# A two-layer encoder trunk with eight experts: passes of 1024 inner features in place of 512, 4096 B rows of gate and up, and banks of sums handed out by count

## The chip, the cores and the metric

The program runs on one core of one Trainium2 chip. The metric is the device time of one execution in microseconds (us), the median over runs; lower is better. A profiled execution gives the trace, from which all rows below are taken.

## The reference

256 tokens of 1024 features pass through two layers in float32. The even layer is a convolution and pooling mixer, then a dense SwiGLU; the odd layer a gated convolution and a spatial gating unit, then eight experts, of which each token takes its best two. All that the change touches lies in the experts:

```python
def swiglu(x, w_gate, w_up, w_down):
    return (jax.nn.silu(x @ w_gate) * (x @ w_up)) @ w_down

def moe_swiglu(x, router, w_gate, w_up, w_down):
    t = x.reshape(-1, d)                                   # 256 x 1024
    top_logits, top_idx = lax.top_k((t @ router).astype(jnp.float32), TOP_K)
    top_w = jax.nn.softmax(top_logits, axis=-1)
    gates = jnp.sum(jax.nn.one_hot(top_idx, N_EXPERTS) * top_w[..., None], axis=1)
    for e in range(N_EXPERTS):                             # w_gate[e], w_up[e]: 1024 x 3584, w_down[e]: 3584 x 1024
        out = out + gates[:, e:e + 1] * swiglu(t, w_gate[e], w_up[e], w_down[e])
```

Behind each sub-layer stand a scaled residual and a layer norm.

## The kernel before

The weights of the experts are 352 MB, read once. They come in chunks of 1 MiB, in the order of a list `plan`, one transfer each on SP's queue (line 133), into a ring of eight buffers named `raw`; the first twenty or so find room in other tiles too and are loaded while the odd layer still computes. A chunk is used in two halves, and its buffer comes free when its last reader is done.

Experts are taken by rank of their token count, with room for `CAPS` = 64, 160, 128, 128, 64, 64, 64, 64 tokens at ranks 0 to 7. The tokens of one are gathered by matmuls with a selection matrix (`gather`, tiles `S`, `tok`) in blocks of 128 (wide), 64 (narrow) or 32 (slim); rank 1 has a wide and a slim block. Wide blocks work in pairs of reduced-precision numbers: ACT rounds a half chunk (`whi`, line 151), DVE takes the rest (`wlo`, line 158), and three matmuls of 512 columns (`wm`) replace one. Narrow and slim blocks use the raw float32 weights; two narrow matmuls fill the array's columns side by side, or four slim ones. A float32 matmul shows as two records in the trace.

`plan` is a list of items ("g", "u" or "d", rank, f), for gate, up and down of the f-th of seven passes of 512 inner features; an item is two chunks. `STARTS` says in which round each rank begins, so that two or three experts are under way at a time: a round takes the gates of its experts, the downs of the round before and the ups.

`project` multiplies the gathered tokens with gate or up into one bank of sums (PSUM, tag "mm", four banks) per block. Then `shaped` (ACT's Silu at line 1298, DVE's product at 1301) empties the bank, `turned` transposes the product on PE (line 1308, tiles `ident`, `fdk` or `sgate`) and `parted` or `copied` (line 1320) brings it back. These follow-ups are no loop of their own: `later(d, ...)` puts them d ticks on, and every half chunk is one tick (`step`), so that they stand between the matmuls of the next items. `down` multiplies with the down rows into four more banks (tag "acc"), over all passes of a rank; `finish` adds the result to the tokens by matmuls (`scatter`, tiles `fak`, `fcs`) and DVE (line 1431). Slim blocks add two quarters of a bank first (`fek`, lines 1284 and 1285).

Ten items before the end (`IF_AT`) all engines come to a branch (line 1463), taken only if some expert has more tokens than room, which these inputs don't have. Before it all that fits into the ring has been issued. The last rank, 7, is alone at the end; its items there are g, u of f = 4, 5 and 6 and the downs, among them rank 3's last.

Of the kernel before, what the change touches and what calls it, by code (L numbers as in the profile page):

```python
# [35 lines left out]
IF_AT = 10  # L36
CARRY_AT = 1
LAST_CUT = 2
AHEAD = {"ft": (0, 50), "fd": (20, 24), "fa": (2, 18), "fc": (3, 48), "fe": (7, 50), "fb": (8, 56), "f0": (9, 18), "f1": (10, 60)}
# [3 lines left out]
RANK_AT = 3  # L43
# [14 lines left out]
STARTS = ((0, 0), (2, 4), (6, 7), (1, 11), (4, 11), (5, 14), (3, 18), (7, 21))  # L58
# [17 lines left out]
def tile_trunk(ctx: ExitStack, tc: tile.TileContext, a: dict, out: bass.AP, caps=CAPS, starts=STARTS,  # L76
# [149 lines left out]
    NFB = FE // 512  # L226
# [47 lines left out]
    for what, p, f in plan:  # L274
        for h in range(2):
            if not any(n == P for _, n in _blocks(caps[p])):
                plain.update((2 * len(chunks), 2 * len(chunks) + 1))
            if what == "d":
                expert(p, md, f * 512 + h * 256, 256, 0, D)
            else:  # L280
                expert(p, mg if what == "g" else mu, h * 512, 512, f * 512, 512)
# [188 lines left out]
    def aggregate(st):  # L470
        mv = small.tile([P, 2], F32, name="ln_mv")
        ve.bn_aggr(mv, st)
        return mv
# [18 lines left out]
    def unit(t, st, fast):  # L492
# [4 lines left out]
        off = small.tile([P, 1], F32, name="ln_off")  # L497
# [577 lines left out]
    clock = {"n": 0, "free": 0}  # L1075

    def later(d, f, *args):
        events.setdefault(clock["n"] + d, []).append((f, args))

    def tick():  # L1080
        clock["n"] += 1
        for f, args in events.pop(clock["n"], ()):
            f(*args)

    def drain():
        while events:
            tick()

    def step():

        tick()
        n = state["use"]
        return use(), raw_half(n)
# [87 lines left out]
    def gather(p, bi):  # L1181
# [14 lines left out]
        def pick(q):  # L1196
            b = bank()
            for k in range(4):
# [5 lines left out]
            if wide:  # L1204
                later(1, split, xg[:, ks, 0:n], xg[:, ks, n:2 * n], b)
            else:
                later(1, first_picked if (p, bi) == (0, 0) else plain_picked, xg, q, b)

        def flip():
            b = bank()  # L1210
            for t in range(2):
                te.transpose(b[:, t * P:(t + 1) * P], G[:, t, :], ident)
            o = Sg[p, bi] = taker(p, wide)
            later(1, se.activation, o.bitcast(F32) if p == last else o, b[:, :T], AF.Copy)

        later(1, pick, 0)
        later(2, pick, 1)
        if (p, bi) != (0, 0):
            later(4, flip)
# [10 lines left out]
    def row0():  # L1230
        i = nth("row0") % 2
        return late()[:, 512 * i:512 * (i + 1)]

    def over_halves(p, mms):
# [3 lines left out]
        for pair in range(2):  # L1238
            got = [(h,) + step() for h in (2 * pair, 2 * pair + 1)] if len(kinds) > 1 else None
            if got is None:  # L1240
                for h in (2 * pair, 2 * pair + 1):
                    mms[kinds[0]](h, 0, *step())
                continue
            for bi in (1, 0) if pair == 0 else (0, 1):
# [3 lines left out]
    def project(what, p, f):  # L1248
        bs = [bank() for _ in blocks[p]]

        def wide_mm(h, bi, w, raw):
            for j in range(2):
                k = 2 * h + j
                l = Xg[p, bi][:, k, :]
                wm(bs[bi], l[:, 0:P], l[:, P:2 * P], w[0][:, j, :], w[1][:, j, :], k == 0, k == DB - 1)

        def narrow_mm(h, bi, w, raw):

            for j in range(2):
                k = 2 * h + j  # L1260
                for c in range(2):
                    mm(bs[bi][64 * c:64 * c + 64, 0:256], Xg[p, bi][:, k, :], raw[:, j, 256 * c:256 * c + 256],
                       k == 0, k == DB - 1)

        def slim_mm(h, bi, w, raw):


            for j in range(2):
                for c in range(2):
                    at = 64 * j + 32 * c  # L1270
                    mm(bs[bi][at:at + 32, 0:256], Xg[p, bi][:, 2 * h + j, 0:32], raw[:, j, 256 * c:256 * c + 256],
                       h == 0, h == 3)

        over_halves(p, {P: wide_mm, 64: narrow_mm, 32: slim_mm})
        for bi, (base, n) in enumerate(blocks[p]):
            later(1, shaped, p, f, what, bi, bs[bi] if n == P else bs[bi][:, 0:256])

    def shaped(p, f, what, bi, v):
        n = v.shape[1]
        slim = blocks[p][bi][1] == 32  # L1280
        if slim:
            i = 512 + 5 * T * (nth("sums32") % 2)
            t = own()[0:64, i:i + T]
            se.activation(t, v[64:P], AF.Copy)
            ve.tensor_tensor(t, v[0:64], t, op=OP.add)
            v = t
        if what == "g":
            if p == 0:
                s = mop.tile([P, n], F32, name="sgate", bufs=1)
            elif n == 512:  # L1290
                s = row0()
            else:
                i = 4 + nth("sgate") % 4
                s = late()[:, n * i:n * (i + 1)]
            if slim:
                s = s[0:64]
            sgate[p, f, bi] = s
            se.activation(s, v, AF.Silu)  # L1298
            return
        s = sgate.pop((p, f, bi))  # L1300
        ve.tensor_tensor(s, v, s, op=OP.mult)  # L1301
        later(1, turned, p, f, bi, s)

    def turned(p, f, bi, s):
        b = bank()
        m, n = s.shape
        for k in range(n // P):
            te.transpose(b[:, k * m:(k + 1) * m], s[:, k * P:(k + 1) * P], ident[:m, :m])  # L1308
        later(1, parted if n == 512 else copied, p, f, bi, b[:, 0:n // P * m])

    def parted(p, f, bi, v):
        y = mop.tile([P, 4, 2 * P], F32R, name="mh", bufs=2)
        split(y[:, :, 0:P], y[:, :, P:2 * P], v.rearrange("p (k s) -> p k s", k=4))
        mh.setdefault((p, f), {})[bi] = y

    def copied(p, f, bi, v):

        y = part_of(fy, "fb", 8, [256], F32) if p else mop.tile([P, 256], F32, name="mh0", tag="mh", bufs=2)
        y = y[:, 0:v.shape[1]]
        ve.tensor_copy(y, v)  # L1320
        mh.setdefault((p, f), {})[bi] = y
# [3 lines left out]
    def down(p, f):  # L1325
        rows = mh.pop((p, f))
        spill = spills[p]
        for bi, (_, n) in enumerate(blocks[p]):
            if f == 0 or spill[bi]:
                macc[p, bi] = [bank("mm" if spill[bi] else "acc")[:, 0:256 if n == 32 else 512]  # L1330
                               for _ in range(2 if n == P else 1)]

        def ends_of(bi, j):
            return (f == 0 or spill[bi]) and j == 0, (f == NFB - 1 or spill[bi]) and j == 3

        def wide_mm(j, bi, w, raw):
            l = rows[bi][:, j, :]
            for h in range(2):
                s = slice(h * 512, (h + 1) * 512)
                wm(macc[p, bi][h], l[:, 0:P], l[:, P:2 * P], w[0][:, 0, s], w[1][:, 0, s], *ends_of(bi, j))  # L1340

        def narrow_mm(j, bi, w, raw):

            n = blocks[p][bi][1]
            at = (j % 2 * 2 + j // 2) * n
            for c in range(P // n):
                mm(macc[p, bi][0][n * c:n * c + n, :], rows[bi][:, at:at + n], raw[:, 0, 8 * n * c:8 * n * (c + 1)],
                   *ends_of(bi, j))

        over_halves(p, {P: wide_mm, 64: narrow_mm, 32: narrow_mm})  # L1350
        if f == NFB - 1 and p == last:
            return
        for bi in range(len(blocks[p])):
            if spill[bi]:
                later(1, spilled, p, f, bi, macc[p, bi])
# [12 lines left out]
    def finish(p, bi):  # L1368
# [4 lines left out]
        if blocks[p][bi][1] < P:  # L1373
            later(d, settled, p, bi)
            k = 64 // blocks[p][bi][1]
            for i in range(2 * k):
                later(d + 3 + (3 - k) * i, scatter_few, p, bi, i // k, i % k)
            return
        for h in range(2):
            later(d + 4 * h, settle, p, bi, h)  # L1380
            for t in range(2):
                later(d + 4 * h + 3 + t, scatter, p, bi, t, h)
# [31 lines left out]
    def scatter(p, bi, t, h):  # L1414
        b = bank()
        for i, y in enumerate(parts[p, bi, h]):
            mm(b, Sg[p, bi][:, t * P:(t + 1) * P], y, i == 0, i == 1)
        later(1, taken, p, t, half(h), b)

    def scatter_few(p, bi, t, i):  # L1420

        n = blocks[p][bi][1]
        for h in range(2):
            b, c = bank(), 64 // n * h + i
            r, b = slice(n * c, n * c + n), b[:, 0:8 * n]
            mm(b, Sg[p, bi][r, t * P:(t + 1) * P], parts[p, bi][r, :], True, True)
            later(1, taken, p, t, slice(8 * n * c, 8 * n * c + 8 * n), b)
# [6 lines left out]
    at = len(passes)  # L1434
    for n, g in reversed(list(enumerate(passes))):
        for p in [p for p, f in reversed(g) if n and f == 0]:
            at = min(at, n)
            for bi in reversed(range(len(blocks[p]))):
# [176 lines left out]
```

## Time and profile before

| | |
|---|---|
| median of 3 runs (lowest, highest) | 1310.31 us (1309.09, 1310.47) |
| profiled execution: its own time | 1309.43 us |
| its span, first to last instruction | 1307.7 us, mean granted clock 0.986 |
| instructions | 19372 |
| busy share of the span: PE, PEld, DVE, ACT, POOL | 96%, 67%, 55%, 39%, 2% |
| DMA | 421.17 MB, mean 322 GB/s |

PE is TensorE's matmuls, PEld its loads of weights, DVE VectorE, ACT ScalarE, POOL GpSimd, SP the engine that issues the transfers. Busy is time with an instruction at work; the ends of matmuls are modelled, so start-to-start distances say more than durations. PEclk is the granted clock of TensorE, 1.00 for 2.4 GHz and 0.50 for 1.2. The span is 1.7 us shorter than the execution's time, which holds the launch too.

### The profile page before, as it was taken

How to read it: one execution, taken by the hardware profiler on the slowest of the kernel's cores; microseconds unless marked ns; L12 is line 12 of the kernel's file. 1: busy time of each engine (PE TensorE's matmuls, PEld its weight loads, DVE VectorE, ACT ScalarE, POOL GpSimd, SP SyncE). 2: the span in 40 equal slices, each digit the busy share in tenths (PEclk: the TensorE clock that was granted, in tenths of full speed). 3: DMA queues.
4: the chain of work that ended last, by engine and by line, in shares of the span. 5: the costliest groups of instructions: out<-in, count | busy, mean ns of one | idle time of the engine just before them, and what ended most of it. 6: DMA issues, size and time to landing. Idle time of an engine off the chain costs nothing. (4 is left out here: it accounts for less than half of the span.)

```text
span 1307.7 us, 19372 instructions
## 1 busy us (share of the span) xinstructions
PE 1255.8 (96%) x7585; PEld 870.8 (67%) x7585; DVE 712.9 (55%) x1105; ACT 511.9 (39%) x726; POOL 31.8 (2%) x69
## 2 busy tenths in 40 slices
PE   7989999999999999999999999999999999999795
PEld 6848888888777666767765566565556567666451
DVE  4997666667984255555534334434335566544333
ACT  4246555546442144434342233333334244443210
POOL 4000000001000001000000000000000000000000
PEclk8999999999999999999999999999999999999898
DMA  8425755276879999899999999999999999999994
GB/s 294 168 80 177 254 182 178 66 254 194 325 269 345 376 393 394 316 387 393 390 374 345 386 397 378 353 378 390 394 397 394 394 393 394 393 394 394 390 336 174
DMA packets 195803, 421.17 MB, mean 322 GB/s; under 512 B 6816, under 2 KB 43368, under 8 KB 195704
## 3 DMA queue, kind: packets, MB, share of 16 engines
q1 hardware_dynamic: 194200, 414.58, 85.8%
q0 software_dynamic: 1504, 5.28, 1.2%
q8 instruction: 61, 1.00, 0.3%
q14 instruction: 38, 0.31, 0.1%
HBM read 418.78 MB, written 1.05 MB: 321 GB/s over the span
## 5 line engine op out<-in xcount | busy, mean ns | idle before, releaser
L158 DVE TENSOR_TENSOR wlo<-raw,whi 128x1024 fp32r<-128x1024 f32 x354 | 417.4, 1221 | 167.2 <-ACT whi L151 150.2
L151 ACT ACTIVATE whi<-raw 128x1024 fp32r<-128x1024 f32 x354 | 353.1, 1049 | 169.6 <-DMA raw<-in_odd_moe_w_up 72.4
L98 PE MATMUL mm<-whi,xgw 128*128 128x512 f32 x672 | 216.8, 404 | 0.0
L98 PEld LDWEIGHTS mm<-whi,xgw 128*128 128x128 f32 x672 | 122.5, 190 | 44.9 <-issue 15.7
L98 PE MATMUL mm<-raw,f1k 128*64 128x256 f32 (+1 forms) x1344 | 134.4, 386 | 0.0
L98 PE MATMUL mm<-wlo,xgw 128*128 128x512 f32 x336 | 132.2, 393 | 0.3 <-DVE wlo L158 0.3
L98 PE MATMUL mm<-big,whi 128*128 128x512 f32 (+1 forms) x448 | 129.3, 368 | 1.8 <-ACT whi L151 1.8
L98 PE MATMUL mm<-raw,fek 128*64 128x256 f32 x896 | 108.5, 390 | 6.8 <-PEq L1463 6.8
L98 PE MATMUL acc<-whi,mh 128*128 128x512 f32 (+1 forms) x344 | 108.2, 402 | 0.0
L98 PEld LDWEIGHTS mm<-raw,f1k 128*64 128x64 f32 (+1 forms) x1344 | 72.8, 128 | 52.3 <-issue 17.4
L1298 ACT ACTIVATE fdk<-mm 128x256 f32<-128x256 f32 (+1 forms) x49 | 23.2, 473 | 183.1 <-PE mm L98 183.1
L98 PEld LDWEIGHTS mm<-raw,fek 128*64 128x64 f32 x896 | 62.6, 139 | 45.4 <-issue 19.6
L98 PE MATMUL mm<-big,wlo 128*128 128x256 f32 x384 | 92.5, 282 | 0.0
L98 PE MATMUL acc<-raw,fbs 128*64 128x512 f32 (+1 forms) x560 | 91.8, 512 | 0.0
L1301 DVE TENSOR_TENSOR fdk<-mm,fdk 128x256 f32<-128x256 f32 (+1 forms) x49 | 26.4, 538 | 117.9 <-PE mm L98 117.9
L98 PEld LDWEIGHTS mm<-big,whi 128*128 128x128 f32 x448 | 75.1, 193 | 13.3 <-ACT whi L151 2.0
L98 PEld LDWEIGHTS acc<-whi,mh 128*128 128x128 f32 (+1 forms) x344 | 61.9, 187 | 23.8 <-ACT whi L151 10.0
L98 PEld LDWEIGHTS mm<-wlo,xgw 128*128 128x128 f32 x336 | 63.8, 190 | 14.9 <-DVE wlo L158 0.7
L98 PEld LDWEIGHTS mm<-big,wlo 128*128 128x128 f32 x384 | 69.0, 191 | 3.7
L98 PE MATMUL acc<-wlo,mh 128*128 128x512 f32 x168 | 65.5, 390 | 0.0
L98 PEld LDWEIGHTS acc<-raw,fbs 128*64 128x64 f32 (+1 forms) x560 | 28.5, 125 | 52.2 <-issue 48.0
L98 PE MATMUL acc<-whi,ffh 128*128 128x512 f32 x176 | 55.6, 396 | 0.0
(286 smaller groups left out, 1299.6 us busy)
## 6 DMA issues: line engine op xcount, KB each, us to landing
raw<-in_odd_moe_w_gate SPq DMA_DIRECT2D x110, 1024.0 KB, 11.7
raw<-in_odd_moe_w_up SPq DMA_DIRECT2D x110, 1024.0 KB, 11.4
raw<-in_odd_moe_w_down SPq DMA_DIRECT2D x109, 1024.0 KB, 11.5
raw<-in_even_ffn_w_gate SPq DMA_DIRECT2D x11, 1024.0 KB, 5.5
raw<-in_even_ffn_w_up SPq DMA_DIRECT2D x11, 1024.0 KB, 8.2
raw<-in_even_ffn_w_down SPq DMA_DIRECT2D x11, 1024.0 KB, 6.9
raw<-in_odd_w_in SPq DMA_DIRECT2D x10, 1024.0 KB, 14.6
raw<-in_even_w_in SPq DMA_DIRECT2D x5, 1024.0 KB, 9.2
```

The costliest lines, as they stand in the source:

```text
L98: te.matmul(o, lhsT, rhs, start=start, stop=stop)
L151: se.activation(his[n], r, AF.Copy)
L158: ve.tensor_tensor(los[n], r, his[n].bitcast(F32), op=OP.subtract)
L1298: se.activation(s, v, AF.Silu)
L1301: ve.tensor_tensor(s, v, s, op=OP.mult)
```

## The change

Passes take 1024 inner features (`FBLOCKS`: three of 1024 and one of 512), so a rank has four passes instead of seven, and `STARTS` is rewritten in rounds of that length. A chunk of gate or up is 256 rows of 4096 B instead of 512 rows of 2048 B, but in the last pass; chunks stay 1 MiB, and their number and sum stay. An item is four chunks (two in the last pass). A wide block takes two banks in `project`, a narrow one matmuls of 512 columns instead of 256, a slim one too. `later` names the banks that a follow-up will need; it waits in `due` while more than four would be out. The branch stands seven items before the end.

```diff
-IF_AT = 10
+IF_AT = 7
-RANK_AT = 3
+RANK_AT = 1
-STARTS = ((0, 0), (2, 4), (6, 7), (1, 11), (4, 11), (5, 14), (3, 18), (7, 21))
+STARTS = ((0, 0), (2, 2), (6, 4), (1, 6), (4, 6), (5, 8), (3, 10), (7, 12))
+FBLOCKS = ((0, 1024), (1024, 1024), (2048, 1024), (3072, 512))
...
-        for h in range(2):
+        f0, nf = FBLOCKS[f]
+        for h in range(nf // 256):
...
             else:
-                expert(p, mg if what == "g" else mu, h * 512, 512, f * 512, 512)
+                rows = D * 256 // nf
+                expert(p, mg if what == "g" else mu, h * rows, rows, f0, nf)
...
-    def later(d, f, *args):
-        events.setdefault(clock["n"] + d, []).append((f, args))
-
-    def tick():
+    due = deque()
+    def later(d, f, *args, banks=0):
+        events.setdefault(clock["n"] + d, []).append((f, args, banks))
+    def take(n=1):
+        clock["banks"] += n
+        assert clock["banks"] <= 4
+    def frees(f, *args, n=1):
+        def done():
+            f(*args)
+            take(-n)
+        events.setdefault(clock["n"] + 1, []).append((done, (), -n))
+    def tick(kept=0):
         clock["n"] += 1
-        for f, args in events.pop(clock["n"], ()):
+        new = events.pop(clock["n"], [])
+        for f, args, banks in new:
+            if banks < 0:
+                f(*args)
+        due.extend(e for e in new if e[2] >= 0)
+        while due and clock["banks"] + due[0][2] + kept * (due[0][2] > 0) <= 4:
+            f, args, banks = due.popleft()
             f(*args)
...
     def project(what, p, f):
-        bs = [bank() for _ in blocks[p]]
+        nf = FBLOCKS[f][1]
+        kb, half_f = 1024 // nf, nf // 2
+        n_banks = sum(nf // 512 if n == P else 1 for _, n in blocks[p])
...
         def wide_mm(h, bi, w, raw):
-            for j in range(2):
-                k = 2 * h + j
+            for j in range(kb):
+                k = kb * h + j
                 l = Xg[p, bi][:, k, :]
-                wm(bs[bi], l[:, 0:P], l[:, P:2 * P], w[0][:, j, :], w[1][:, j, :], k == 0, k == DB - 1)
+                for c, b in enumerate(sums(bi)):
+                    s = slice(512 * c, 512 * c + 512)
+                    wm(b, l[:, 0:P], l[:, P:2 * P], w[0][:, j, s], w[1][:, j, s], k == 0, k == DB - 1)
...
-    def shaped(p, f, what, bi, v):
+    def shaped(p, f, what, bi, vs):
...
         s = sgate.pop((p, f, bi))
-        ve.tensor_tensor(s, v, s, op=OP.mult)
-        later(1, turned, p, f, bi, s)
+        if slim:
+            v = vs[0]
+            for i in range(nf // 2 // T):
+                t, c = own()[0:64, 512 + 5 * T * i:][:, 0:T], slice(T * i, T * (i + 1))
+                se.activation(t, v[64:P, c], AF.Copy)
+                ve.tensor_tensor(t, v[0:64, c], t, op=OP.add)
+                ve.tensor_tensor(s[:, c], t, s[:, c], op=OP.mult)
+        else:
+            for i, v in enumerate(vs):
+                c = slice(v.shape[1] * i, v.shape[1] * (i + 1))
+                ve.tensor_tensor(s[:, c], v, s[:, c], op=OP.mult)
+        mh.setdefault((p, f), {})[bi] = []
+        for i in range(len(vs)):
+            c = slice(vs[i].shape[1] * i, vs[i].shape[1] * (i + 1))
+            later(1 + i, turned, p, f, bi, s[:, c], banks=1)
```

What stands on PE where the experts begin, with the gather of rank 0 first (`xg` are its gathered tokens, 64x256 the columns of weights and of the moving operand, `ident,sgate` the transposes of its products, `mh` the products in `down`). Before:

```order
L98 MATMUL mm<-S,tok 128x64 x16
L98 MATMUL mm<-raw,xg_3677 64x256 x12
L1212 MATMUL mm<-ident,S 128x128 x2
L98 MATMUL mm<-raw,xg_3677 64x256 x24
L1308 MATMUL mm<-ident,sgate 128x128 x2
L98 MATMUL mm<-raw,xg_3677 64x256 x28
L98 MATMUL acc<-raw,mh_3781 64x512 x2
L1308 MATMUL mm<-ident,sgate 128x128 x2
L98 MATMUL acc<-raw,mh_3781 64x512 x6
L98 MATMUL mm<-raw,xg_3677 64x256 x32
L98 MATMUL acc<-raw,mh_3839 64x512 x2
L1308 MATMUL mm<-ident,sgate 128x128 x2
```

And in the changed kernel:

```order
L100 MATMUL mm<-S,tok 128x64 x16
L100 MATMUL mm<-raw,xg_3677 64x512 x6
L1240 MATMUL mm<-ident,S 128x128 x2
L100 MATMUL mm<-raw,xg_3677 64x512 x28
L1362 MATMUL mm<-ident,sgate 128x128 x4
L100 MATMUL mm<-raw,xg_3677 64x512 x26
L100 MATMUL mm<-whi,xg_3677 64x512 x4
L100 MATMUL acc<-whi,mh_3799 64x512 x2
L1362 MATMUL mm<-ident,sgate 128x128 x4
L100 MATMUL mm<-S,tok 128x128 x8
L100 MATMUL acc<-whi,mh_3799 64x512 x2
```

The same columns stand in fewer and longer stretches, with four transposes at a time instead of two.

What stands on PE behind the end of an up of rank 1 (first row: its slim block; then rank 4's up, 64 columns of `f1k`; `ident,fdk` 128x128 are the transposes of rank 1's wide block and then of other ranks, the 128x64 ones those of the slim block). Before:

```order
L98 MATMUL mm<-raw,f1k 32x256 x8
L98 MATMUL mm<-raw,f1k 64x256 x4
L1308 MATMUL mm<-ident,fdk 128x128 x4
L1308 MATMUL mm<-ident,fdk 128x64 x2
L98 MATMUL mm<-raw,f1k 64x256 x12
L98 MATMUL mm<-raw,fek 64x256 x4
L1308 MATMUL mm<-ident,fdk 128x128 x2
L98 MATMUL mm<-raw,fek 64x256 x12
L98 MATMUL mm<-raw,f1k 32x256 x8
```

And in the changed kernel:

```order
L100 MATMUL mm<-raw,f1k 32x512 x4
L100 MATMUL mm<-raw,f1k 64x512 x2
L1362 MATMUL mm<-ident,fdk 128x128 x4
L1362 MATMUL mm<-ident,sgate 128x64 x4
L100 MATMUL mm<-raw,f1k 64x512 x2
L1362 MATMUL mm<-ident,fdk 128x128 x4
L100 MATMUL mm<-raw,f1k 64x512 x12
L100 MATMUL mm<-raw,fek 64x256 x4
L1362 MATMUL mm<-ident,fdk 128x128 x4
L100 MATMUL mm<-raw,fek 64x256 x12
L100 MATMUL mm<-raw,f1k 32x512 x4
```

The wide block's transposes come in two groups, and those of the slim block stand after the first of them, four instead of two.

What stands on PE at the end of the stream (`fek`: rank 7's gate and up, `fbs`: its downs, `fak`: the scatter of rank 3, `total,ident`: the tokens' own share). Before:

```order
L98 MATMUL mm<-raw,fek 64x256 x16
L1308 MATMUL mm<-ident,fdk 128x128 x2
L98 MATMUL mm<-raw,fek 64x256 x28
L98 MATMUL acc<-raw,fbs 64x512 x2
L1308 MATMUL mm<-ident,fdk 128x128 x2
L98 MATMUL acc<-raw,fbs 64x512 x6
L98 MATMUL acc<-total,ident 128x512
L98 MATMUL acc<-raw,fbs 64x512 x2
L98 MATMUL acc<-total,ident 128x512
L98 MATMUL acc<-raw,fbs 64x512 x2
L98 MATMUL mm<-total,ident 128x512 x2
L98 MATMUL acc<-raw,fbs 64x512 x12
```

And in the changed kernel:

```order
L100 MATMUL acc<-raw,fbs 64x512 x2
L100 MATMUL mm<-fak 128x512 x2
L1362 MATMUL mm<-ident,fdk 128x128 x2
L100 MATMUL acc<-raw,fbs 64x512 x14
L100 MATMUL acc<-total,ident 128x512
L100 MATMUL acc<-raw,fbs 64x512 x2
L100 MATMUL acc<-total,ident 128x512
L100 MATMUL acc<-raw,fbs 64x512 x2
L100 MATMUL mm<-total,ident 128x512 x2
L100 MATMUL acc<-raw,fbs 64x512 x20
```

The last downs are 40 matmuls in place of 24. Over the whole of the experts, without the branch that isn't taken, PE has 283 stretches of one kind of matmul (wide, narrow of 256 or of 512 columns, slim, gather, transposes, scatter), and had 367.

## Rows read from the trace of the kernel before

**Rows 1.** The page of the kernel before, parts 1 and 3.

```profile
PE 1255.8 (96%) x7585; PEld 870.8 (67%) x7585; DVE 712.9 (55%) x1105; ACT 511.9 (39%) x726; POOL 31.8 (2%) x69
...
q1 hardware_dynamic: 194200, 414.58, 85.8%
```

**Rows 2.** Stages of the experts: length, busy per engine (instructions), PEclk, DMA share, GB/s.

```profile
402.00:873.00 471.00, 465.68 (x3065) 300.30 (x3066) 213.23 (x271) 165.63 (x219) 5.88 (x4) 1.00 1.00 373
873.00:1242.00 369.00, 357.17 (x2190) 225.33 (x2188) 179.80 (x207) 134.83 (x163) 1.11 (x2) 0.98 1.04 393
1242.00:1250.00 8.00, 8.00 (x58) 5.38 (x56) 3.17 (x3) 4.17 (x5) 0.00 (x0) 0.85 0.45 156
1250.00:1288.00 38.00, 37.75 (x219) 18.27 (x219) 8.03 (x14) 1.97 (x4) 0.00 (x0) 1.00 1.00 381
```

**Rows 3.** Waits of SP's queue, 350 to 1308 us: total, times, longest.

```profile
SPq L133 <- PE mm L98: 334.5, 146, 8.6
SPq L133 <- PE acc L98: 126.8, 54, 9.2
```

**Rows 4.** Timeline of PE: start us, us, operation, count, as expert 0 begins.

```profile
408.74 5.40 PE L98 MATMUL mm<-raw,xg 128*64 128x256 f32 x48
414.07 0.44 PE L1308 MATMUL mm<-ident,sgate 128*128 128x128 f32 x2
...
424.49 7.08 PE L98 MATMUL mm<-raw,xg 128*64 128x256 f32 x64
431.40 1.03 PE L98 MATMUL acc<-raw,mh 128*64 128x512 f32 x4
```

**Rows 5.** GB/s of the DMA engines in 40 slices of 1050 to 1100 us.

```profile
GB/s 392 395 393 387 387 387 385 390 387 387 385 388 387 387 385 390 383 398 380 398 410 410 419 410 400 405 400 405 383 387 385 390 385 388 383 390 397 369 387 387
```

**Rows 6.** Timeline of SP's queue, transfers issued shortly before and in that stretch.

```profile
1058.98 5.51 SPq L133 DMA_DIRECT2D raw<-in_odd_moe_w_gate  x4
1068.24 3.69 SPq L133 DMA_DIRECT2D raw<-in_odd_moe_w_down  x4
```

**Rows 7.** Timelines of ACT and PE, 1190 to 1212 us.

```profile
1196.56 2.01 ACT L151 ACTIVATE whi<-raw 128x1024 fp32r<-128x1024 f32 x2 [6.11 <-DMA raw<-in_odd_moe_w_gate]
1202.43 0.44 PE L1308 MATMUL mm<-ident,fdk 128*128 128x128 f32 x2 [2.31 <-DVE fdk L1301]
```

**Rows 8.** Two windows of 15 us, columns as in rows 2.

```profile
1200.00:1215.00 15.00, 12.69 (x66) 9.20 (x66) 8.47 (x9) 5.91 (x8) 0.00 (x0) 0.89 1.03 402
1230.00:1245.00 15.00, 7.69 (x46) 4.64 (x44) 0.92 (x3) 0.00 (x0) 0.00 (x0) 0.66 0.96 369
```

**Rows 9.** Timeline of PE with 64 columns of weights: 512 and 256 wide.

```profile
929.38 3.65 PE L98 MATMUL mm<-raw,fbs 128*64 128x512 f32 x16
932.86 3.60 PE L98 MATMUL acc<-raw,fbs 128*64 128x512 f32 x16
```

**Rows 10.** Timeline of DVE behind an up of expert 1.

```profile
943.18 0.69 DVE L1301 TENSOR_TENSOR fdk<-mm,fdk 128x512 f32<-128x512 f32 x1 [4.87 <-PE mm L98]
944.63 0.42 DVE L1285 TENSOR_TENSOR fek<-mm,fek 64x256 f32<-64x256 f32 x1 [0.75 <-ACT fek L1284]
945.08 0.42 DVE L1301 TENSOR_TENSOR fdk<-fek,fdk 64x256 f32<-64x256 f32 x1
```

**Rows 11.** Timeline of PE at 697 us; PE's waits, 400 to 1290 us.

```profile
697.51 0.44 PE L1308 MATMUL mm<-ident,fdk 128*128 128x128 f32 x2 [2.37 <-DVE fdk L1301]
PE mm L1308 <- DVE fdk L1301: 10.4, 11, 2.4
```

**Rows 12.** Timelines of PE and of SP's queue about the branch.

```profile
1239.19 9.69 PE L98 MATMUL mm<-raw,fek 128*64 128x256 f32 x64 [6.78 <-PEq L1463]
1247.58 1.02 SPq L133 DMA_DIRECT2D raw<-in_odd_moe_w_gate  x2
```

**Rows 13.** End of the stream: PE's last long stretch; GB/s in 1 us slices, 1250 to 1290.

```profile
1286.37 5.37 PE L98 MATMUL acc<-raw,fbs 128*64 128x512 f32 x24
GB/s 406 389 414 393 383 387 389 387 391 393 365 381 391 389 381 389 393 377 391 385 395 416 408 397 418 414 397 393 422 414 406 381 430 401 410 410 148 41 0 0
```

More of the change, by code (lines that the diff above doesn't have):

```diff
@@ L1197, in pick @@
             b = bank()
+            take()
             for k in range(4):
@@ L1248, in project, with sums @@
     def project(what, p, f):
-        bs = [bank() for _ in blocks[p]]
+        nf = FBLOCKS[f][1]
+        kb, half_f = 1024 // nf, nf // 2
+        n_banks = sum(nf // 512 if n == P else 1 for _, n in blocks[p])
+        bs = []
+        def sums(bi):
+            if not bs:
+                bs.extend([bank() for _ in range(nf // 512 if n == P else 1)] for _, n in blocks[p])
+                take(n_banks)
+            return bs[bi]
         def wide_mm(h, bi, w, raw):
-            for j in range(2):
-                k = 2 * h + j
+            for j in range(kb):
+                k = kb * h + j
@@ L1320, in copied @@
         ve.tensor_copy(y, v)
-        mh.setdefault((p, f), {})[bi] = y
+        mh[p, f][bi].append(y)
     macc, ysum = {}, {}
     def down(p, f):
+        nf = FBLOCKS[f][1]
+        for bi, (_, n) in enumerate(blocks[p]):
+            while len(mh[p, f][bi]) < (nf // 512 if n == P else 1):
+                tick()
         rows = mh.pop((p, f))
         spill = spills[p]
[L1328 to L1331, printed above, removed]
+        n_banks = sum((2 if n == P else 1) * spill[bi] for bi, (_, n) in enumerate(blocks[p]))
@@ L1333, in ends_of, with sums @@
+        new = [bi for bi in range(len(spill)) if f == 0 or spill[bi]]
+        def sums(bi):
+            if new:
+                for i in new:
+                    n = blocks[p][i][1]
+                    macc[p, i] = [bank("mm" if spill[i] else "acc")[:, 0:256 if n == 32 else 512]
+                                  for _ in range(2 if n == P else 1)]
+                take(n_banks)
+                new.clear()
+            return macc[p, bi]
         def ends_of(bi, j):
-            return (f == 0 or spill[bi]) and j == 0, (f == NFB - 1 or spill[bi]) and j == 3
+            return (f == 0 or spill[bi]) and j == 0, (f == NFB - 1 or spill[bi]) and j == nf // P - 1
@@ L1433, in tile_trunk @@
     gathers = {}
[L1434 to L1438, printed above, removed]
-                at -= 1
-                gathers[("u",) + passes[at][-1]] = (p, bi)
+    at = len(plan)
+    for n, p in reversed([(plan.index(("g", p, 0)), p) for p, n0 in starts if n0]):
+        at = min(at, n - 1)
+        for bi in reversed(range(len(blocks[p]))):
+            at -= 1
+            gathers[plan[at]] = (p, bi)
     total_at = plan.index(("d", starts[0][0], NFB - 1)) - 3
@@ L1505, in carry @@
         F[t, h] = bank("acc" if t else "mm")
+        take(0 if t else 1)
         mm(F[t, h], ident, total[0][:, t, half(h)], True, False)
@@ L1545, in tile_trunk @@
             n = len(macc[last, bi])
-            ysum[last, bi] = [row0() for _ in range(n)]
+            ysum[last, bi] = [row0(i) for i in range(n)]
             if n == 1:
```

147 lines of the change are left out of this document (78 added, 69 removed).

## Prediction

> **What bounds the kernel now.** I read the page first, then windows over the experts (402 to 1288 us), then the waits of SP's queue and of PE, and last the timelines where one of them stands.
>
> The page has PE at 96% of the span and the main queue's packets at 85.8% [rows 1]. In the windows both are nearly full at once [rows 2]: to 873 us PE works 465.68 of 471 us and the transfers run at 373 GB/s with some gaps; from 873 to 1242 PE works 357.17 of 369 us and the transfers have a share of 1.04, which is no gap at all, at 393 GB/s. Which of the two waits for the other? SP's queue waits 334.5 and 126.8 us for matmuls to free a buffer [rows 3], while PE's largest wait for anything but the branch sums to 10.4 us [rows 11]. Thus PE is the bound, with the transfers so close behind that they catch it now and then, as at 1196 us, where ACT waits 6.11 us for gate rows and PE then stands 2.31 us [rows 7].
>
> Is a busy PE one that works? The start-to-start distances say so: 64 narrow records of 256 columns without a break take 431.40 - 424.49 = 6.91 us, 0.108 each. A stretch of 48 that is cut off by transposes takes 414.07 - 408.74 = 5.33, where 48 x 0.108 would be 5.18 [rows 4]. So a change from one kind of matmul to another costs 0.15 us, and that hides in "busy".
>
> **The change part by part.** The sum is made against the profiled execution (1309.43 us, 0.9 below the median of 1310.31).
>
> *Fewer stretches.* All experts, 283 stretches of one kind on PE for 367: 84 changes x 0.15 = **-12.6**. Nothing else hides them, since PE is what is waited for.
>
> *Wider matmuls.* 16 records of 512 columns take 932.86 - 929.38 = 3.48 us [rows 9], 32 of 256 take 3.46 (half of the 6.91). The halved number of narrow matmuls and weight loads brings **0**: each column still passes once, and the loads lie under the matmuls before. The Trainium skill sees the loads otherwise ("TensorE: Matmul & The Clock Gate", Back-to-back issue gap and LDWEIGHTS): the spacing in a stream is set by load and matmul together, and a load takes its columns over 1.2, 53 ns for 64; by that the 960 records that go would give back up to 51 us, and the sum would be 1242. The rows of the two widths, equal to 0.02 us, speak against it.
>
> *4096 B rows.* While gate rows land, the transfers move 385 to 390 GB/s; in the stretch at 1075 to 1085 us, when the downs issued at 1068 land, 400 to 419 [rows 5, 6]. Taken as 387 and 408, a chunk of 1 MiB takes 2.71 and 2.57 us. By 402 us some 15 chunks have landed (the bytes of rows 2 are 321 chunks of 336), so 209 of gate and up are left, of which 32 keep 2048 B: 177 x 0.14 = 25 us less transfer. That isn't the kernel's gain, since PE is the bound; it takes away what the transfers cost PE. At 1196 to 1207 us that is the wait of 2.31 and the clock that falls after it: the window at 1200 has a mean clock of 0.89, 1.65 us lost [rows 7, 8]. **-4.0**. It stays hidden as long as the ring is ahead: PE needs some 870 us for the stage, the transfers 336.4 MB less those 25 us, about 830.
>
> *Transposes of the slim block.* Behind an up of rank 1 DVE now has two products of 0.69 us for the wide block and then twice an addition and a product of 0.42 each [rows 10]. The wide block ends one slim group (0.87, eight records side by side in fours) before the slim block; so DVE is done 0.1 + 2 x 0.69 + 4 x 0.42 - 0.87 = 2.3 us behind the slim block's end. PE has in hand two matmuls of rank 4 (0.87), a change (0.15) and four transposes (0.6): 1.6. It waits 0.7 in three passes: **+2**. Behind it on PE stands the rest of rank 4's up, so all of it counts.
>
> *Transposes without cover.* Where a narrow up is followed by rank 1's gate or up, two ticks pass at once and nothing stands between its last matmul and its transposes. That was so in seven places and is in four; one cost 2.37 us [rows 11]. Without the late one at 1202 us the ten waits there sum to 8.1; the four that stay wait for a product of 0.69 instead of 0.42, 0.27 more each. I count 3 x 0.8 - 4 x 0.27 = 1.3, and some for waits before wide transposes that come half as often: **-2**. Not covered by any row; the bounds are 0 and -6.
>
> *Banks by count.* A wide item holds two of four banks, rank 1's three. Each is emptied by ACT or DVE within 0.6 to 0.7 us of the item's end, while the next item fills others: **0**; this is the rival below.
>
> *The branch and the end.* PE stands 6.78 us and SP issues again at 1247.58, 8.4 behind PE [rows 12]. Behind the branch SP then had 14 chunks, 8 of gate and up: 8 x 2.71 + 6 x 2.57 = 37.1; now 16, 4 of them with 2048 B: 41.7. The last landed at about 1287.8, 40.2 behind the first issue, so now 44.8. PE's matmuls ended at 1286.37 + 5.37 = 1291.74 [rows 13], 44.2 behind that issue; two more chunks of narrow work (3.48) make 47.7, and as much less stands before the branch. The transfers still come in time: **0**.
>
> *Nothing:* fewer, wider evacuations on ACT and DVE (39% and 55% busy), fewer additions for rank 4, the shorter list of small tiles.
>
> Sum: -12.6 - 4.0 + 2 - 2 = **-16.6**, 1292.8 for the profiled execution and 1293.7 for the median; I say **1294**. Its own range: the change of kind between 0.12 and 0.16 (-10 to -13.5), waits +4 to -6: 1287 to 1303.
>
> **The rivals.**
>
> *A, strided rows gain nothing.* The downs are one contiguous MiB, gate and up rows lie 14336 B apart, so 408 GB/s may be owed to that. Then from 873 us on the transfers bound as before, and only what PE gains up to there counts: 471 of 840 us of the stage, 0.56 x 14.6 = 8, less 1 at the slim block, and the end takes 16 chunks at up to 2.71: about **1304**. For it: no row has 4096 B rows with a stride. Against: the rate steps with the size of row and nothing else in view. The Trainium skill has an account that ends the same way ("DMA: Bandwidth & Descriptors", Where 436 GB/s comes from: the HBM side binds at about 358 GB/s per core, whatever the packets); the 393 and 400 to 419 of the rows are above that figure, so I give it little.
>
> *B, slower: waits for banks.* Each of rank 1's eight gates and ups needs three of the four banks at its first matmuls. If one of them is still to be emptied by DVE behind rounded weights, PE stands like at 697 us (2.37 us) and loses 1.65 by the clock: 4.0 a time. From four such waits on the gain is gone, eight make **1326**. For it: DVE did come 2.4 us late there. Against: the item before has always ended by then, and its product is first in DVE's order.
>
> *C, the changes of kind aren't saved.* If the 0.15 is the wait of whatever follows, it goes to the next matmul: 1309.4 - 4.0 + 0.9 = **1306**.
>
> *D, loads of weights on the path.* PEld's 870.8 us over 7585 loads are 0.115 us each [rows 1]; 960 fewer, two side by side, would take 55 us: **1239**. Rows 9 speak against it.
>
> **How the numbers follow.** Forecast 0.68, A 0.12, B 0.10, C 0.08, D 0.02. Within 0.2% (2.6 us) a measurement of this kernel cannot tell from no change. The range 1285 to 1308 takes the forecast's own, A and C, and some 2 us below for waits that vanish. Faster: nearly all of the forecast, A, half of C, D, 0.82; same: the rest of C and of the forecast's upper end, with bank waits of one to three, 0.07; slower: 0.11.
>
> **What would show it.** In the changed kernel PE's busy share stays at 98% or more over the experts, and the branch lies some 20 us earlier (1210; 3.5 of it moved). The transfers show gaps between 500 and 1200 us and 405 GB/s or more without them. Behind rank 1's ups the transposes of 128x64 wait 0.5 to 1 us three times. No 2 us wait near the end of rank 3. The forecast fails if the GB/s beside gate rows stay at 387 (A), if PE's waits for DVE or ACT at first matmuls sum to over 15 us (B), or if PE has the same 0.15 per record group at equal busy time (C).

## The result and the profile after

The changed kernel takes **1294.78 us** (median of 4 runs, 1293.29 to 1296.50) where the kernel before takes 1310.39: a ratio of 0.989, 95% interval 0.9878 to 0.9902, or 15.6 us less. I had said 1294. The number came out; the account of it did not, as the runs below show.

The page of the changed kernel (busy time, share of the span, instructions; then the queue of the transfers):

```profile
PE 1242.3 (96%) x6433; PEld 799.2 (62%) x6433; DVE 713.2 (55%) x1066; ACT 514.6 (40%) x705; POOL 32.4 (3%) x69
...
q1 hardware_dynamic: 145048, 414.58, 84.3%
```

A quarter of the packets and 1152 records of matmuls are gone, the bytes are the same, and the shares look as they did [rows 1]. Its windows over the experts, columns as in [rows 2]:

```profile
402.00:873.00 471.00, 466.03 (x2389) 261.20 (x2388) 220.84 (x245) 174.83 (x212) 6.27 (x4) 1.00 0.97 376
873.00:1200.00 327.00, 324.97 (x1677) 187.68 (x1676) 169.20 (x184) 126.96 (x146) 1.11 (x2) 1.00 1.03 403
1200.00:1211.00 11.00, 10.20 (x49) 4.24 (x47) 2.07 (x3) 0.60 (x1) 0.00 (x0) 1.00 1.03 409
1211.00:1218.00 7.00, 0.34 (x4) 0.21 (x4) 0.69 (x1) 0.00 (x0) 0.00 (x0) 0.59 1.03 404
1218.00:1234.00 16.00, 16.00 (x64) 5.33 (x63) 0.19 (x1) 1.88 (x3) 0.00 (x0) 0.86 0.72 274
1234.00:1271.00 37.00, 34.67 (x166) 16.47 (x166) 10.78 (x14) 4.31 (x6) 0.00 (x0) 0.95 1.03 402
```

The transfers run at 403 GB/s where they ran at 393, and PE is at 99% of the stretch up to the branch. But they still have no gap from 873 to 1218 us (share 1.03): both are full at once, as before. The timeline of PE (start, duration, idle time before in brackets):

```profile
399.48 3.68 PE L100 MATMUL mm<-S,tok 128*128 128x64 f32 x32
...
708.87 1.06 PE L100 MATMUL mm<-raw,f1k 128*32 128x512 f32 x8
709.87 0.72 PE L100 MATMUL mm<-whi,xgw 128*128 128x512 f32 x2
...
726.64 0.34 PE L1362 MATMUL mm<-ident,sgate 64*128 64x64 f32 x2 [0.41 <-DVE sgate L1347]
...
1203.48 6.23 PE L100 MATMUL mm<-raw,fek 128*64 128x512 f32 x28
...
1217.82 16.26 PE L100 MATMUL mm<-raw,fek 128*64 128x512 f32 x64 [6.66 <-DVEq L1534]
1234.01 0.72 PE L100 MATMUL acc<-whi,mh 128*128 128x512 f32 x2
...
1238.26 0.66 PE L1362 MATMUL mm<-ident,fdk 128*128 128x128 f32 x4 [1.97 <-DVE fdk L1351]
```

The wait near 1202 us [rows 7] has no counterpart. A new one, of 1.97, stands behind the branch. SP's queue says why, in its timeline and in its waits (us in total, times, longest) behind 1205 us:

```profile
1204.60 5.53 SPq L135 DMA_DIRECT2D raw<-in_odd_moe_w_up  x4
1227.63 1.02 SPq L135 DMA_DIRECT2D raw<-in_odd_moe_w_down  x2
```

```profile
SPq L1534 <- SPq L1534: 16.3, 5, 5.2
```

At the branch SP waits until all eight loads under way have landed (16.3 us in five waits; the transfers' rate falls to nothing before it issues again), and only then issues rank 3's downs. PE has used the eight chunks by 1234; these downs must land, be rounded by ACT and subtracted by DVE, and DVE's product for the transposes at 1238.26 stands behind that. So PE loses 1.97 and 0.35 us there and, as the clock falls behind it, 1.8 more (0.95 over the 37 us of the last window).

From PE's first expert matmul to its last, 885.5 us became 873.2: 12.4 less. The other 2.5 of the profile's 14.9 us lie ahead of the experts, where nothing was changed (gather at 402.02, now 399.48). In the other traces of this study that point lies between 398.9 and 402.4, so it is scatter.

### The profile page after: what moved, and what is told of

It reads as the page before. It is cut to its first block, busy times and chain, and to the rows that moved or that the text cites. A ratio compares the mean times of both kernels' runs of the same rounds, so it can differ in the third digit from the quotient of the medians.

```text
span 1292.8 us, 17007 instructions
## 1 busy us (share of the span) xinstructions
PE 1242.3 (96%) x6433; PEld 799.2 (62%) x6433; DVE 713.2 (55%) x1066; ACT 514.6 (40%) x705; POOL 32.4 (3%) x69
## 3 DMA queue, kind: packets, MB, share of 16 engines
q1 hardware_dynamic: 145048, 414.58, 84.3%
## 5 line engine op out<-in xcount | busy, mean ns | idle before, releaser
L153 ACT ACTIVATE whi<-raw 128x1024 fp32r<-128x1024 f32 x354 | 357.1, 1052 | 215.3 <-DMA raw<-in_odd_moe_w_up 90.7
L100 PE MATMUL mm<-whi,xgw 128*128 128x512 f32 x672 | 213.2, 398 | 0.0
L100 PE MATMUL mm<-raw,f1k 128*64 128x512 f32 (+3 forms) x768 | 130.6, 546 | 0.0
L100 PE MATMUL acc<-whi,mh 128*128 128x512 f32 (+1 forms) x352 | 112.8, 414 | 0.0
L100 PE MATMUL mm<-raw,fek 128*64 128x512 f32 (+1 forms) x512 | 104.6, 554 | 6.7 <-DVEq L1534 6.7
L100 PEld LDWEIGHTS mm<-raw,f1k 128*64 128x64 f32 (+1 forms) x768 | 40.2, 127 | 67.8 <-issue 60.7
L1338 ACT ACTIVATE fdk<-mm 128x512 f32<-128x512 f32 (+1 forms) x37 | 21.1, 573 | 151.4 <-PE mm L100 150.7
L100 PEld LDWEIGHTS mm<-raw,fek 128*64 128x64 f32 x512 | 35.5, 139 | 61.3 <-issue 56.6
L100 PE MATMUL acc<-wlo,mh 128*128 128x512 f32 (+1 forms) x184 | 70.8, 417 | 0.4 <-DVE wlo L160 0.4
L1351 DVE TENSOR_TENSOR fdk<-mm,fdk 128x512 f32<-128x512 f32 (+1 forms) x37 | 24.4, 662 | 82.6 <-PE mm L100 82.6
```

The costliest lines, as they stand in the source:

```text
L100: te.matmul(o, lhsT, rhs, start=start, stop=stop)
L153: se.activation(his[n], r, AF.Copy)
L1338: se.activation(s[:, n * i:n * (i + 1)], v, AF.Silu)
L1351: ve.tensor_tensor(s[:, c], v, s[:, c], op=OP.mult)
```

## The experiments

Medians, with the ratio to the kernel before on the same chip and its 95% interval.

**The new bank code alone** (`banks512`): passes of 512 and the old tables in the changed code.

```diff
-IF_AT = 7
+IF_AT = 10
...
-STARTS = ((0, 0), (2, 2), (6, 4), (1, 6), (4, 6), (5, 8), (3, 10), (7, 12))
-
-FBLOCKS = ((0, 1024), (1024, 1024), (2048, 1024), (3072, 512))
+STARTS = ((0, 0), (2, 4), (6, 7), (1, 11), (4, 11), (5, 14), (3, 18), (7, 21))
+
+FBLOCKS = tuple((512 * i, 512) for i in range(7))
...
```

> The changed code with seven passes of 512 and the old rounds: only the way in which banks are handed out is new; 368 stretches on PE, as before (367). My theory (the bank code costs nothing, the gain is fewer stretches and larger packets): 1310 us, within 3. Rival (the hand-out by count makes or removes waits): a share of the 15.5 us shows here already, below 1306, or it costs, above 1314.

Measured: 1313.53 us for 1309.45, ratio 1.0032 (1.0019 to 1.0044). That is just above my 1310 within 3 and just below the 1314 of the rival: the bank code isn't free, it costs 2.5 to 5.8 us here. One place of several on PE, and then the same place in the kernel before:

```profile
804.25 2.81 PE L100 MATMUL mm<-raw,f1k 128*64 128x256 f32 x24
809.09 0.41 PE L1362 MATMUL mm<-ident,fdk 128*128 128x128 f32 x2 [2.03 <-DVE fdk L1351]
809.34 2.38 PE L100 MATMUL mm<-S,tok 128*128 128x64 f32 x16
```

```profile
806.42 2.00 PE L98 MATMUL mm<-S,tok 128*128 128x64 f32 x16
...
810.83 0.44 PE L1308 MATMUL mm<-ident,fdk 128*128 128x128 f32 x2 [0.16 <-DVE fdk L1301]
```

Before, gathers stood in front of and among these ups, and their transposes waited 0.16 us for DVE. Now a gather comes behind the transposes (by the code it waits in `due` for a bank; no row shows that), so they have less cover and wait 2.03. With passes of 512 the bank code gives none of the 15.6 us.

**The packet alone undone** (`rows2048`), and its control (`halves4096`):

```diff
+            elif n_moe // 2 <= c < len(chunks) - LAST_CUT and (k, f) == (2, D) and "down" not in v.tensor.name:
+                for i in range(2):
+                    sy.dma_start(raws[c][:, :, i * 512:(i + 1) * 512], v[:, :, i * 512:(i + 1) * 512])
```

The control has `raws[c][:, i:i + 1, :], v[:, i:i + 1, :]` in its last line.

> The changed kernel, but each chunk of gate and up comes as two transfers of 512 columns each, so its packets are 2048 B again; nothing else differs. My theory: PE keeps its 283 stretches, but from 873 us on the transfers can't follow it: at about 390 instead of 403 to 406 GB/s the stretch to 1200 us takes some 10 us longer, less what the ring holds ahead: 1300 to 1306 us, with waits of ACT and PE for gate and up rows near the end. Rival 1 (the transfers are hidden, packets don't matter): 1295 us. Rival 2 (all of the gain is the packets'): 1310 us.

> Control for the run before: two transfers per chunk of gate and up again, but each of 128 rows of 4096 B. My theory: the number of transfers costs nothing, 1295 us within 2. Rival (twice as many transfers, not the packet, is what costs): as much as the run with 2048 B.

Measured: 2048 B 1309.05 us (1.0006, 0.9996 to 1.0015); halves of 4096 B 1296.17 (0.9899, 0.9885 to 0.9914). Two transfers for one cost 1.4 us, which the intervals can't tell from nothing; against this control the packet costs 12.9 us, most of what the change had brought. Rival 2 named the time, and my 1300 to 1306 was too low. PE, in the kernel with 2048 B:

```profile
1000.39 0.73 PE L100 MATMUL mm<-whi,xgw 128*128 128x512 f32 x2 [1.26 <-ACT whi L156]
...
1203.44 0.74 PE L100 MATMUL mm<-whi,xgw 128*128 128x512 f32 x2 [1.37 <-ACT whi L156]
...
1246.27 1.22 PE L100 MATMUL acc<-whi,mh 128*128 128x512 f32 x2 [3.92 <-ACT whi L156]
```

and its window, 394 GB/s without a gap:

```profile
873.00:1200.00 327.00, 323.06 (x1657) 185.57 (x1658) 164.26 (x180) 123.33 (x142) 1.12 (x2) 0.99 1.04 394
```

Against the changed kernel its matmuls lag 1.6 us at 795 (as they did when the experts began), 5.3 at 1005, 8.0 at 1205 and 12.3 at 1246. The first two steps are waits of ACT for gate or up rows, with the clock behind the one at 1000. The last is a wait for rank 3's downs, the first loads behind the branch, which SP issues at 1239.96 here and at 1227.63 in the changed kernel. The control waits there too (us in total, times, longest), so this is not all the packet's:

```profile
PE acc L100 <- ACT whi L156: 2.6, 1, 2.6
```

PE had the time that fewer stretches give; the transfers took it back, up to the branch and at it.

**The packet alone done** (`before4096`): the kernel before, fetching other weights (256 rows of 1024 columns) into the same chunk, so that only the packets differ; what it computes of gate and up is not the reference's.

```diff
+            elif c >= n_moe // 2 and k == 4:
+                sy.dma_start(raws[c].rearrange("p (k a) f -> p k (a f)", a=2), src(other=True))
...
+            if other:
+                r0, nr, c0, ncol = r0 // 2, nr // 2, min(c0, FE - 2 * ncol), 2 * ncol
```

> The kernel before, in which the transfers of gate and up alone are changed: each fetches 256 rows of 4096 B instead of 512 of 2048 B into the same 1 MiB, so that these weights are the wrong ones, and everything else (367 stretches, banks, order) stays. Theory P, as I predicted (PE is the bound, the packets take away one late wait): 1304 to 1306 us. Theory T (with 2048 B the transfers hold the kernel at 1309 from some 900 us on, whatever PE could do; with 4096 B what binds is PE with its 367 stretches, between the runs of 328 and of 415): 1298 to 1303. Theory Q (packets alone, changes of kind cost nothing): 1294 to 1297.

Measured: 1301.99 us for 1309.40, ratio 0.9946 (0.9932 to 0.9959): theory T. Its transfers in the window, and PE where the late gate rows had stopped it before [rows 7]:

```profile
873.00:1200.00 327.00, 325.76 (x2030) 205.89 (x2027) 166.94 (x195) 124.03 (x152) 1.11 (x2) 1.00 1.02 400
```

```profile
1197.67 0.38 PE L1312 MATMUL mm<-ident,fdk 128*128 128x128 f32 x2
1197.81 0.71 PE L98 MATMUL mm<-whi,xgw 128*128 128x512 f32 x2
```

No wait is left there. With these runs the change comes apart in two, the packets and the rest:

| us | 2048 B | 4096 B |
|---|---|---|
| passes of 512 | 1309.4 | 1302.0 |
| passes of 1024 | 1309.0 | 1294.8 |

The lower row differs from the upper one in the fewer stretches, but also in the bank code and in the place of the branch. This rest is worth nothing alone, and 7 us once the packets are there; the packets are worth 7 us alone and 14 with the rest (13 with `halves4096` in the last cell, which has two transfers for a chunk as `rows2048` has). In one trace each, from PE's first expert matmul to its last, the four are 885.5 and 879.0, 884.4 and 873.2 us: the same order, with smaller differences.

**The changes of kind put back, three ways, with 4096 B.** `split_ones` takes the four transposes of a group apart, each a half chunk behind the other (the first hunk); `split_turns` has them two by two (2 for 1 there); `changes` takes rank 1's blocks in turns for each half chunk (the last hunk).

```diff
+        def rest(k0):
+            for k in range(k0, min(k0 + 1, n // P)):
...
+            if k0 + 1 < n // P:
+                later(1, rest, k0 + 1)
...
-            for bi in (1, 0) if pair % 2 == 0 else (0, 1):
-                for h, w, raw in got:
+            for h, w, raw in got:
+                for bi in (1, 0):
```

> The same with two transposes and two: 328 stretches, 45 more than the changed kernel. My theory: 5.4 to 6.8 us more, 1300 to 1302. Rival: 1295 to 1297.

> The changed kernel, packets of 4096 B, but the four transposes of a group stand one by one, each behind another half chunk: 415 stretches on PE in place of 283, the same matmuls and transfers. My theory (a change of kind costs 0.12 to 0.15 us and nothing hides it, packets or not): 132 x 0.12 to 0.15 = 16 to 20 us more than the changed kernel, 1311 to 1315. Rival (the gain of the change is that of the packets, and PE has time for the changes of kind once the transfers are faster): 1295 to 1299.

> The changed kernel with rank 1's wide and slim block taken in turns for every half chunk instead of every second: the same matmuls, 393 stretches instead of 283, all 110 more between wide and slim. My theory (a change of kind costs 0.12 to 0.15 us wherever it stands): 13 to 16.5 us more, 1308 to 1311. Rival (the 0.15 only delays what has time, or is the wait of whatever follows): 1295 to 1299. With over 1314 something else than the change of kind is hit.

Measured: 1295.11 (0.9898, 0.9884 to 0.9912), 1306.63 (0.9984, 0.9975 to 0.9992) and 1331.10 us (1.0164, 1.0150 to 1.0177). The first is the rival's, the second between the theories, the third above both. The traces tell why. PE with the transposes one by one, in a wide stretch and in a narrow one:

```profile
718.67 0.39 PE L100 MATMUL mm<-wlo,xgw 128*128 128x512 f32 x1
718.90 0.38 PE L1363 MATMUL mm<-ident,fdk 128*128 128x128 f32 x2
719.03 0.71 PE L100 MATMUL mm<-whi,xgw 128*128 128x512 f32 x2
719.58 0.39 PE L100 MATMUL mm<-wlo,xgw 128*128 128x512 f32 x1
...
1216.67 1.08 PE L100 MATMUL mm<-raw,fek 128*64 128x512 f32 x4
1217.68 0.33 PE L1363 MATMUL mm<-ident,fdk 128*128 128x128 f32 x1
1217.93 1.08 PE L100 MATMUL mm<-raw,fek 128*64 128x512 f32 x4
1218.95 0.33 PE L1363 MATMUL mm<-ident,fdk 128*128 128x128 f32 x1
```

In the narrow stretch four records and a transpose come every 1.27 us, where 4 x 0.215 (32 records take 7.02 us there, 16 take 3.58) and 0.11 are 0.97: 0.15 for each of the two changes, as I had it. In the wide stretch the three wide records and two transposes from 718.67 to 719.58 take 0.91 us, which is what they take without a change (0.23 + 0.46 and 2 x 0.11): the changes there are free. So the price belongs to some pairs of kinds. Besides, the delayed transposes took the wait behind the branch away (1.97 and 1.8 us by the clock in the changed kernel, 1.74 alone with pairs, none one by one), which gave some 2 us back with pairs and 4 one by one. For `split_ones` 11.9 + 4 over 132 changes is 0.12 each, for `split_turns` 0.3 + 2 over 45 is 0.05: the price depends on where the changes stand.

In `changes` another cost was hit, which I had not seen in the edit:

```profile
724.25 1.05 PE L100 MATMUL mm<-raw,f1k 128*32 128x512 f32 x4
725.23 0.73 PE L100 MATMUL mm<-whi,xgw 128*128 128x512 f32 x2
```

Four slim records take 0.98 us where eight take 1.00 (708.87 to 709.87 above): only with two half chunks together do four slim matmuls fill the columns side by side. Slim stretches grew from 41.0 to 67.7 us, wide ones from 365.2 to 375.6 with 61 more of them, 0.17 each. The sum of the two, 37.1, is what the run lost (36.3): here what is added to PE shows in full.

**The width of a matmul** (`width256`): 480 more matmuls of half the columns.

```diff
-                for c in range(2):
-                    mm(sums(bi)[0][64 * c:64 * c + 64, 0:half_f], Xg[p, bi][:, k, :],
-                       raw[:, j, half_f * c:half_f * (c + 1)], k == 0, k == DB - 1)
+                for q in range(0, half_f, 256):
+                    for c in range(2):
+                        mm(sums(bi)[0][64 * c:64 * c + 64, q:q + 256], Xg[p, bi][:, k, :],
+                           raw[:, j, half_f * c + q:half_f * c + q + 256], k == 0 and q == 0, k == DB - 1 and q == half_f - 256)
```

> The changed kernel, but each gate or up matmul of 64 columns of weights and 512 columns is two of 256; 287 stretches, 480 more matmuls (960 records). My theory (the width costs nothing, only the changes of kind do): 1295 us, within 1.5. Rival (a load of weights of 64 columns stands on the path, 0.05 us for each of the 960 records): 1320 or more, up to 1346.

Measured: 1296.38 us (0.9902, 0.9889 to 0.9915). 56 records of 256 columns:

```profile
1205.83 6.26 PE L100 MATMUL mm<-raw,fek 128*64 128x256 f32 x56
```

That is 6.26 us busy, where 28 of 512 have 6.23 (1203.48 above). The rule of the Trainium skill that I had weighed ("TensorE: Matmul & The Clock Gate", Back-to-back issue gap and LDWEIGHTS) does not set the time here: 960 loads more don't show (1.6 us, with intervals that overlap).

**Where the branch stands** (`if5`, first hunk) and **what stands behind it** (`down_first`, second hunk):

```diff
-IF_AT = 7
+IF_AT = 5
...
         plan.insert(len(plan) - 2, plan.pop(len(plan) - 5))
+        plan.insert(len(plan) - 7, plan.pop(len(plan) - 6))
```

> The changed kernel with the branch five items before the end instead of seven, so that behind it the first half of the eight buffers holds rank 3's last downs and the chunks loaded afterwards are narrow ones. My theory (where it now stands, the branch costs a wait of 2.9 us for the first chunk loaded behind it, rounded by ACT and DVE, and 1.8 by the clock after it, which the kernel before didn't have): 4 to 5 us less, 1290 to 1291. Rival (the branch costs the same wherever it is, or the fewer chunks behind it find less to cover the drained ring): 1294 to 1299.

> The changed kernel with rank 3's last downs one item earlier, before the up of rank 7's third pass, so that their two chunks are among the eight loaded before the branch, which stays where it is; a correct kernel. Theory (the wait of 2.0 and 0.35 us for the first chunk loaded behind the branch, and the clock that falls after it, 1.8, are what the changed kernel loses there): 3 to 4.5 us less, 1290 to 1292. Rival (behind the branch the transfers bind whatever the order, as in the run with the branch five items before the end): 1294 to 1297.

Measured: `if5` 1300.48 us (0.9935, 0.9922 to 0.9947), a miss: 5.7 more than the changed kernel in place of 4 to 5 less. PE says what I had left out:

```profile
1219.65 1.94 PE L100 MATMUL mm<-raw,fek 128*64 128x512 f32 x8 [0.72 <-DMA raw<-in_odd_moe_w_up]
1222.11 1.94 PE L100 MATMUL mm<-raw,fek 128*64 128x512 f32 x8 [0.53 <-DMA raw<-in_odd_moe_w_up]
...
1235.37 1.12 PE L1362 MATMUL mm<-ident,fdk 128*128 128x128 f32 x4 [6.21 <-DVE fdk L1351]
1242.39 1.19 PE L100 MATMUL acc<-whi,mh 128*128 128x512 f32 x2 [5.90 <-PEq L1534]
```

Rank 7 alone is narrow: PE uses a chunk in 1.74 us, one lands every 2.5, and without the branch ahead of them its eight chunks come late. Where the branch stands in the changed kernel, its 6.66 us are also the time in which the ring fills. DVE's product (the wait of 6.21) then stands behind the rounding of downs that are late too, and the branch costs 5.90 besides.

`down_first` leaves the branch and takes rank 3's downs among the eight chunks: **1291.75 us** (1289.85 to 1293.90), ratio 0.9859 (0.9842 to 0.9875), below the changed kernel's interval. It beats both kernels.

```profile
1220.10 9.85 PE L100 MATMUL mm<-raw,fek 128*64 128x512 f32 x32 [6.63 <-DVEq L1535]
1229.88 0.73 PE L100 MATMUL acc<-whi,mh 128*128 128x512 f32 x2
...
1259.36 1.94 PE L100 MATMUL acc<-raw,fbs 128*64 128x512 f32 x8 [0.35 <-DMA raw<-in_odd_moe_w_down]
```

The wait at the downs is gone, and the last ones now catch PE at 1259 us, by 0.35 in one place: behind the branch PE and the transfers are now close to each other.

**Larger packets still**: downs of two neighbouring rows to a partition (`downs8192`), and gate and up too from other weights (`all8192`, whose experts are not the reference's).

```diff
-            return v.rearrange("(k p) f -> p k f", p=P)
+            return v.rearrange("(p k) f -> p k f" if w is md else "(k p) f -> p k f", p=P)
...
-            te.transpose(b[:, k * m:(k + 1) * m], s[:, k * P:(k + 1) * P], ident[:m, :m])
+            cols = s[:, 2 * P * (k // 2):2 * P * (k // 2 + 1)].rearrange("m (p i) -> m i p", i=2)[:, k % 2, :]
+            te.transpose(b[:, k * m:(k + 1) * m], cols, ident[:m, :m])
```

> The changed kernel with downs of 8192 B: partition p takes the rows 2p and 2p+1 of a chunk, and the transposes take every second column to fit; a correct kernel. Theory T (behind 900 us the transfers still bind the changed kernel): a third of the chunks at some 412 instead of 405 GB/s (worked out from 394 at 2048 B and 405 at 4096 B, a fixed share per packet), 1 to 2 us less: 1293 to 1294. Theory P (PE binds it): 1295 within 1. Rival (a read of every second column costs PE): above 1297.

> The same, and gate and up as well in 8192 B: 128 rows of 2048 columns into the same 1 MiB, so that these weights are the wrong ones. Theory T: 412 instead of 405 GB/s over some 340 us and shorter waits at the end: 4 to 6 us less, 1289 to 1291. Theory P: 1295 within 1.

Measured: 1294.65 (0.9884, 0.9868 to 0.9899) and 1292.40 us (0.9872, 0.9857 to 0.9887). The first cannot be told from the changed kernel; the second is 2.4 below it, short of what theory T asked, and the intervals of the two ratios just overlap. Its windows:

```profile
873.00:1200.00 327.00, 326.00 (x1677) 189.95 (x1676) 168.78 (x184) 126.33 (x146) 1.11 (x2) 1.00 1.00 405
1000.00:1100.00 100.00, 100.00 (x507) 61.44 (x505) 62.71 (x71) 44.04 (x50) 0.00 (x0) 1.00 1.01 413
```

The share is down to 1.00 and PE at 99.7%: with these packets PE bounds the stretch, and the wait of 1.97 us behind the branch is down to 0.2. Both kernels also pay for the transposes:

```profile
1205.96 0.74 PE L1363 MATMUL mm<-ident,fdk 128*128 128x128 f32 x4
1206.63 5.80 PE L100 MATMUL mm<-raw,fek 128*64 128x512 f32 x26
```

Four take 0.67 us with every second column, and 0.59 without; over the experts the transposes grew from 25.1 to 28.9 us (waits left out), which may hide what the larger downs gave.

## Why the prediction was right, and where it was not

*"Thus PE is the bound, with the transfers so close behind".* This step failed. PE's busy share and its few waits can't tell a bound from a tie: with 99% on PE and no gap in the transfers from 873 us on, both were bounds. `rows2048` and the changed kernel have the same work on PE and differ by 14.3 us (12.9 against the control).

*"That isn't the kernel's gain, since PE is the bound": -4.0.* Mis-sized and misread. `before4096` measures -7.4 (-5.4 to -8.9 by its interval), of which the wait at 1202 and the clock behind it are 4.0, as I had them, and none is left; two smaller waits of the kernel before are gone too (0.70 us at 1171, 0.27 at 1199), and what made the rest is not shown. The 25 us less transfer (some 32 by the shares of the queue's packets in both pages) were, besides, the condition of the next term.

*Fewer stretches, -12.6.* Right in the mechanism, too large, and not free-standing. Summed over all stretches, what each takes beyond its matmuls at constant pace (those left out that a wait or the clock prolongs) goes from 45.7 to 36.5 us: -9.2, 0.11 each. Narrow and slim stretches cost the 0.15 that I had read off [rows 4], wide ones between slim ones 0.17 (`changes`), transposes among wide ones nothing. The medians give -7.2 with 4096 B for the rest of the change, in which the wait behind the branch, and whatever the bank code costs, is counted too.

*Wider matmuls, 0.* Right (`width256`).

*Slim block, +2; uncovered transposes, -2.* Three waits of 0.4 us, as at 726.64, sum to 1.2, where I had 0.7 each. PE's other waits for DVE before transposes, the one behind the branch left out, sum to 6.0 us (0.8 of it for another operation on DVE, line 1503), for 8.1: -2.1.

*Banks by count, 0.* With passes of 512 the code costs 2.5 to 5.8 us (`banks512`); with 1024 it wasn't measured apart. The rival of waits for banks at the first matmuls didn't come: the changed trace has one wait of 0.5 us for ACT, before a gather, and none before a first matmul.

*The branch and the end, 0.* Failed by some 4 us: I had counted the chunks behind the branch, and they do come in time for the end, but not which of them is first and how many steps stand between its landing and PE. `down_first` takes 3.0 of it back by the medians.

Of the marks I had set, the branch stands at 1211 (21 us earlier), PE is at 99%, and the rate reaches 403 to 409. Gaps between 500 and 1200 us were forecast, and from 900 on there are none. No wait of 2 us was to be left near the end of rank 3, and one of 1.97 stands behind the branch, at rank 3's last downs.

The parts as measured sum to about -13.4 (-9.2 - 7.4 + 1.2 - 2.1 + 4.1), where the trace has -12.4 over the experts and the medians have -15.6. That -16.6 came so near is luck: the stretches were priced 3 us too high and the branch 4 too low, the packets' part was 3 too small, and 2.5 us of the profiled difference lie ahead of the experts. The upper end of the forecast's own range doesn't follow from the bounds that it names: -10 and waits of +4 give some 1300, not 1303.

Rival A (strided rows no faster) is refuted by the 403 and 406 GB/s; its logic, that from 873 us on the transfers hold whatever PE gains, was right for packets of 2048 B. Rival C is refuted by `split_ones`, which pays for the changes that are put back, and D by `width256`.

## What to carry to other kernels

When two resources are both within a per cent of full, don't ask which is the bound; ask what each part of the change is worth with and without the other, and run all four combinations. Measure a part against a control that differs in nothing else: here two transfers for one brought a wait of their own. A price per change of kind has to be read for each pair of kinds that the change touches. A branch that lets the transfers run dry cost most here through what is first behind it: let the chunks with the longest way from landing to use be loaded ahead of it.

## What the runs showed of the hardware

Of packets, from 1000 to 1100 us, in stretches with hardly a gap: 394 GB/s in the kernel before, with nearly two thirds of the bytes in packets of 2048 B and the rest in 4096 B; 406 in the changed kernel, with a tenth in 2048 B; 413 in `all8192`, with 8192 B alone. The pages say what a packet costs besides its bytes: 194200 packets took 85.8% of 1307.7 us and 145048 took 84.3% of 1292.8, 32 us less on each of 16 engines for the same bytes, so some 10 ns for each packet that is saved (an estimate from these rows). The Trainium skill states such a fixed overhead per packet ("DMA: Bandwidth & Descriptors", Why small descriptors are slow); these rates agree in kind. Strided rows (14336 B apart) lose nothing that shows against contiguous ones: with 4096 B alone (`before4096`) two thirds of 40 slices of that stretch have 401 to 413 GB/s, and the contiguous downs before had 400 to 419 [rows 5].

Transposes that read every second column take 0.02 us longer each (0.67 for 0.59 by fours). Changes between transposes and wide matmuls cost PE nothing that shows, those from narrow matmuls to transposes and back 0.15 us each.
